# Tying a chunk's transposes behind the next chunk's gate product on TensorE

## The chip, the cores and the metric

One core of one Trainium2 chip runs the kernel. The metric is the time of one execution on the device, in microseconds; a run's number is a median over executions. TensorE is PE in the profile (its weight loads are PEld), VectorE is DVE, ScalarE is ACT, GpSimd is POOL, and SP is the engine whose queue starts the loads.

## The reference

Two decoder layers on 256 tokens of width 1024, all in float32. The first has two kinds of attention and a dense feed-forward part, the second a gated recurrence and then a mixture of experts. Only the last concerns the change: each token goes to the two best of eight experts, and an expert is a gated feed-forward part of width 3584.

```python
def swiglu(u, w_gate, w_up, w_down):
    return (jax.nn.silu(u @ w_gate) * (u @ w_up)) @ w_down

def moe_swiglu(u, w_router, w_gate, w_up, w_down):
    ...
    for e in range(N_EXPERTS):
        y = swiglu(t, w_gate[e], w_up[e], w_down[e]).astype(F32)
        out = out + gates[:, e:e + 1] * y
```

## The kernel before

**A product in three parts.** float32 values are split into a high and a low part. `mm3` (L100) makes one product out of three matmuls: high by high (L101), high by low weights (L102), low by high weights (L103). `split` (L88, both instructions on L91) makes the parts of a weight tile: ACT copies the raw tile to `w_hi`, then DVE subtracts to get `w_lo`. One `split` covers 128x1024 values. `w_hi` and `w_lo` have four buffers each, the raw tiles that the loads fill have fourteen.

**A chunk.** The experts' part is cut into 56 chunks, `Job`s: eight experts, seven chunks of 512 inner columns each. An expert sees at most 128 tokens in its slots. One chunk does this:

- `gate` (L1160): the slots' rows by the gate weights, through `into` (L1144). Two loads of 2 MB in all, four splits, and six matmuls of 128x512 for each split, 24 in all, into one PSUM tile `acc`. Then ACT takes the SiLU into `sg` (L1163). I call the four splits of a chunk's gate G1 to G4.
- `up` (L1165): the same with the up weights, splits U1 to U4. Then DVE multiplies into `hm` (L1168), which has one buffer.
- `turn` (L1170): four TensorE transposes of `hm` into the PSUM tile `tp` (L1173). ACT copies them into `hh` (L1177), and DVE subtracts into `hl` (L1178). `hh` and `hl` have one buffer each.
- `down` (L1180): `hh` and `hl` by the down weights, splits D1 to D4, 24 matmuls into the two PSUM tiles `pj`, which are summed over the seven chunks of an expert. After an expert's last chunk `add` (L1194) scales the sum into `y` (L1202) on ACT and adds it to the output by an indirect DMA; these steps wait in the list `later` and are taken up in the middle of the next chunk's products (L1155).

**The order.** `run_jobs` (L1258) writes a software pipeline: gate of chunk j+1, `turn` of chunk j, up of chunk j+1, down of chunk j. So the written order on PE is down(j-1), gate(j+1), transposes(j), up(j+1), down(j). Where a new pair of experts begins (chunks 14, 28 and 42, counted from 0) `fresh` gathers the next slots' rows and calls the `turn` of the chunk before in the middle of that, followed at once by its `down`.

The written order is not yet the order of the queues. When the program is built, a planner goes through it with estimated costs and puts an instruction into its engine's queue as soon as the estimate has it ready, with the order of the code as the priority. So an instruction whose data is early may be queued ahead of ones written before it. On the chip each queue then runs in the order it was given. `tc.issue_after(ins)` adds an order to this: whatever its block writes for the engine of `ins` is queued behind `ins`. It is an order of issue and not a wait for the end of `ins`, and it holds on that engine alone.

Of the kernel before, what the change touches and what calls it, by code (L numbers as in the profile page):

```python
# [18 lines left out]
KT = D // P  # L19
# [20 lines left out]
def tile_trunk(  # L40
# [22 lines left out]
    nc = tc.nc  # L63
# [11 lines left out]
    def bank(tag, bufs=2):  # L75
        return psum.tile([P, 512], F32, name=tag, tag=tag, bufs=bufs)
# [5 lines left out]
    def load(shape, pieces):  # L82
        r = raws.tile([P] + shape, F32, name="raw", tag="raw")
        for dst, src in pieces(r):
            nc.sync.dma_start(out=dst, in_=src)
        return r

    def split(view, shape):  # L88
        hi = subs.tile([P] + shape, F32R, name="w_hi", tag="w_hi")
        lo = subs.tile([P] + shape, F32R, name="w_lo", tag="w_lo")  # L90
        split.last = nc.scalar.activation(hi, view, AF.Copy), nc.vector.tensor_sub(lo, view, f32(hi))  # L91
        return hi, lo
# [7 lines left out]
    def mm3(ps, xh, xl, wh, wl, first, last, chk=False):  # L100
        nc.tensor.matmul(ps, lhsT=xh, rhs=wh, start=first, stop=False, skip_group_check=chk)  # L101
        nc.tensor.matmul(ps, lhsT=xh, rhs=wl, start=False, stop=False, skip_group_check=chk)  # L102
        nc.tensor.matmul(ps, lhsT=xl, rhs=wh, start=False, stop=last, skip_group_check=chk)  # L103

    def pair_load(w, c0, c1, k):
        wv = [w_.rearrange("(kt p) c -> p kt c", p=P) for w_ in w]
# [2 lines left out]
    def pair_steps(xh, xl, w, c0, c1, ps, late=False, raw=None, ready={}):  # L109


        box = {}

        def step(k):
            if k % 4 == 0:
                box["r"] = raw if raw and k == 0 else pair_load(w, c0, c1, k)
            if k % 2 == 0:
                box["w"] = ready[k] if k in ready else split(box["r"][:, k % 4:k % 4 + 2], [2, 2, 256])
            wh, wl = box["w"]
            box[k] = wh[:, k % 2], wl[:, k % 2]  # L120
            if not late or k >= KT // 2:
                part(k, 0)
                part(k, 1)
            elif k == KT // 2 - 1:
                for t in range(NT):
                    for j in range(KT // 2):
                        part(j, t)

        def part(k, t):
            mm3(ps[t], xh[:, k, TOK[t]], xl[:, k, TOK[t]], *box[k], k == 0, k == KT - 1)  # L130

        return [(1.3, lambda k=k: step(k)) for k in range(KT)]

    def col_steps(xh, xl, w, c0, ps):

        wv = w.rearrange("(kt p) c -> p kt c", p=P)
        box = {}

        def step(k):
            if k == 0:  # L140
                box["r"] = load([KT, 256], lambda r: [(r, wv[:, :, c0:c0 + 256])])
            if k % 4 == 0:
                box["w"] = split(box["r"][:, k:k + 4], [4, 256])
            wh, wl = box["w"]
            for t in range(NT):
                mm3(ps[:, t * 256:(t + 1) * 256], xh[:, k, TOK[t]], xl[:, k, TOK[t]], wh[:, k % 4], wl[:, k % 4],
                    k == 0 and t == 0, k == KT - 1, chk=True)

        return [(0.65, lambda k=k: step(k)) for k in range(KT)]

    def row_steps(xh, xl, wv, ks, acc, first, last):

        box = {}

        def step(k, t):
            if k % 2 == 0 and t == 0:
                box["r"] = load([2, D], lambda r: [(r, wv[:, k:k + 2, :])])
            if t == 0:
                box["w"] = split(box["r"][:, k % 2], [D])
            wh, wl = box["w"]  # L160
            for c in range(2):
                mm3(acc[t][c], xh[:, k, TOK[t]], xl[:, k, TOK[t]], wh[:, HALF[c]], wl[:, HALF[c]], k == first, k == last)

        return [(1.3, lambda k=k, t=t: step(k, t)) for k in ks for t in range(NT)]
# [115 lines left out]
    def to_T(src, xh, xl, t, k0, k1, scale=None, s0=0, gain=None):  # L280
        for k in range(k0, k1, 4):
            n = min(4, k1 - k)
            ps = bank("tp")
            for i in range(n):
                nc.tensor.transpose(out=ps[:, i * P:(i + 1) * P], in_=src[:, (k + i - s0) * P:(k + i - s0 + 1) * P], identity=ident)
            pv = ps[:, :n * P].rearrange("p (a b) -> p a b", b=P)
            oh, ol = xh[:, k:k + n, TOK[t]], xl[:, k:k + n, TOK[t]]
            if gain is not None:
                for i in range(n):
                    g = cols[:, gain + k + i:gain + k + i + 1]  # L290
                    last = (nc.scalar.activation(oh[:, i], pv[:, i], AF.Copy, scale=g),
                            nc.vector.scalar_tensor_tensor(ol[:, i], pv[:, i], g, f32(oh[:, i]), op0=ALU.mult, op1=ALU.subtract))
            elif scale is None:
                last = nc.scalar.activation(oh, pv, AF.Copy), nc.vector.tensor_sub(ol, pv, f32(oh))  # L294
            else:
                last = (nc.scalar.activation(oh, pv, AF.Copy, scale=scale),
                        nc.vector.scalar_tensor_tensor(ol, pv, scale, f32(oh), op0=ALU.mult, op1=ALU.subtract))
        return last

    def x_tiles():  # L300
        return (xts.tile([P, KT, S], F32R, name="xh", tag="xh"), xts.tile([P, KT, S], F32R, name="xl", tag="xl"))

    def norm_T(hgs, gain, acc, into=None):

        xh, xl = into or x_tiles()
        rs = []
        for t in range(NT):
            for c in range(2):
                nc.vector.tensor_add(h[t][:, HALF[c]], acc[t][c], h[t][:, HALF[c]])
                nc.vector.tensor_mul(hgs[t][:, HALF[c]], h[t][:, HALF[c]], gain[:, HALF[c]])  # L310
            r, pw = rms(t)
            rs.append(r)
            for c in range(2):
                to_T(hgs[t], xh, xl, t, 4 * c, 4 * c + 4)
        return xh, xl, rs, pw
# [45 lines left out]
    with tc.tile_pool(name="att", bufs=2) as att, tc.tile_pool(name="atc", bufs=1) as atc:  # L361
# [7 lines left out]
        xh, xl = x_tiles()  # L369
        last = to_T(h[0], xh, xl, 0, 0, 8, gain=GAIN_A)  # L370
        with behind(last):
            ready = {k: split(first[:, k:k + 2], [2, 2, 256]) for k in (0, 2)}
        with behind(split.last):
            last = to_T(h[1], xh, xl, 1, 0, 8, gain=GAIN_A)
# [248 lines left out]
        xh, xl, rx, pw = norm_T([att.tile([P, D], F32, name="wide", tag="sc") for t in range(NT)], gain_f, acc)  # L623
# [5 lines left out]
    with tc.tile_pool(name="ffn", bufs=2) as ffn:  # L629
# [5 lines left out]
        class Chunk:  # L635
# [4 lines left out]
            def into(self):  # L640
                self.pg = [bank("pj") for _ in range(2)]
                return feature_steps(xh, xl, (ffn_w_gate[0], ffn_w_up[0]), self.ch * 256, self.pg)
# [49 lines left out]
        prev = None  # L692
        for ch in range(NCH):
# [10 lines left out]
            prev = cur  # L704
        prev.down()
        xh, xl, rx, pw = norm_T([ffn.tile([P, D], F32, name="wide", tag="wide") for t in range(NT)], gain_h, acc)
# [427 lines left out]
    class Job:  # L1134
# [9 lines left out]
        def into(self, w):  # L1144
            rows = self.rows()
            ps = [bank("acc", 4) for _ in rows]
            for k0 in (0, 4):
                r = load([4, 512], lambda r: [(r, w[:, k0:k0 + 4, self.ch * 512:(self.ch + 1) * 512])])
                for i in range(0, 4, 2):
                    wh, wl = split(r[:, i:i + 2], [2, 512])  # L1150
                    for j in range(2):
                        k = k0 + i + j
                        for p_, (xh, xl, es) in zip(ps, rows):
                            mm3(p_, xh[:, k, es], xl[:, k, es], wh[:, j], wl[:, j], k == 0, k == KT - 1)
                    if later and k0 + i:  # L1155
                        with tc.issue_after(split.last[0].ins):
                            later.pop(0)()
            return ps
# [99 lines left out]
    def run_jobs(jobs):  # L1258

        prev = None  # L1260
        for job in jobs + [None]:
            if job and job.fresh:
                job.fresh(job.shared, prev.turn)
                prev.down()
                prev = None
            if job:
                job.gate()
            if prev:
                prev.turn()
            if job:  # L1270
                job.up()
            if prev:
                prev.down()
            prev = job

    jobs = []
    for e in range(NE):
# [11 lines left out]
        for ch in range(NCH):  # L1289
            kind = {(0, 0): FirstJob, (NE - 1, NCH - 1): LastJob}.get((e, ch), Job)  # L1290
            jobs.append(kind(
                ch, shared, slice((e % 2) * P, (e % 2 + 1) * P), (moe_w_gate[0, e], moe_w_up[0, e], moe_w_down[0, e]), e % 2,
                fresh if e in (2, 4, 6) and ch == 0 else None))
    run_jobs(jobs)


# [5 lines left out]
    with tc.If(most > P):  # L1302
        ecur = mc.tile([P, 1], F32, name="ecur")
        nc.vector.memset(ecur, 0.0)
        with tc.For_i(0, NE, 1) as e:
# [16 lines left out]
            for src, dst in ((nh, xg2[0]), (nl, xg2[1])):  # L1322
                for k0 in range(0, KT, 4):
                    pt = bank("tp")
                    for i in range(4):
                        k = k0 + i
                        for t in range(NT):
                            nc.tensor.matmul(pt[:, i * P:(i + 1) * P], lhsT=src[t][:, k * P:(k + 1) * P], rhs=oh2[:, t],
                                             start=(t == 0), stop=(t == NT - 1))
# [50 lines left out]
```

## Time and profile before

| | |
|---|---|
| median of 3 runs | 1488.56 us (1488.22 to 1489.09) |
| the profiled execution, its own time | 1489.99 us |
| its span in the profile | 1488.3 us |
| TensorE, matmuls | 1453.3 us busy, 98% of the span |
| TensorE, weight loads | 1216.6 us, 82% |
| VectorE | 1213.9 us, 82% |
| ScalarE | 1035.2 us, 70% |
| DMA | 434.05 MB, mean 292 GB/s |
| granted TensorE clock | 0.996 of full speed, mean |

Matmuls are pipelined and their ends are modelled, so TensorE's busy share says little about how near it is to its limit; the distance from one start to the next says more. The experts' chunks fill the span from about 520 us to its end. A line of the timeline shows the start of an instruction, its length, where it stands in the code, and in brackets how long its engine had been idle and who ended that.

### The profile page before, as it was taken

The numbers are of one execution on the slowest core, as the hardware profiler recorded it, in microseconds if no ns is written. First come the engines' busy times: TensorE is split into PE (matmuls) and PEld (weight loads), VectorE is DVE, ScalarE is ACT, GpSimd is POOL, SyncE is SP. The second block draws the span as 40 slices with busy tenths as digits, with TensorE's granted clock in tenths as the row PEclk, the third lists the DMA queues.
The fourth block names the chain that finished last, engine by engine and source line by source line (L and its number), as shares of the span: only waits on it lengthen the run. The fifth ranks groups of instructions, "written<-read, shape, count | busy, mean of one in ns | idle before, by whom it ended". The sixth has DMA issues, their size and how long they took to land.

```text
span 1488.3 us, 20143 instructions
## 1 busy us (share of the span) xinstructions
PE 1453.3 (98%) x7509; PEld 1216.6 (82%) x7509; DVE 1213.9 (82%) x1460; ACT 1035.2 (70%) x1285; POOL 31.9 (2%) x45
## 2 busy tenths in 40 slices
PE   7999999999999999999999999999999999999996
PEld 6887899998889788888888878888877888887885
DVE  7775656557867899999989888889888888888885
ACT  6655544445766688888878777777777777778774
POOL 1000000000000100000000000000000000000000
PEclk9999999999999999999999999999999999999999
DMA  9933355656454499999999999999999999999971
GB/s 315 369 125 114 128 182 187 186 183 183 142 170 142 143 348 365 384 370 385 379 348 376 356 351 395 360 353 360 374 367 373 381 366 350 356 371 362 391 262 16
DMA packets 209691, 434.05 MB, mean 292 GB/s; under 512 B 7402, under 2 KB 58642, under 8 KB 209586
## 3 DMA queue, kind: packets, MB, share of 16 engines
q1 hardware_dynamic: 207506, 425.77, 79.6%
q0 software_dynamic: 2080, 6.92, 2.3%
q8 instruction: 61, 1.00, 0.3%
q14 instruction: 44, 0.36, 0.1%
HBM read 427.41 MB, written 5.24 MB: 291 GB/s over the span
## 4 chain that ended last, share of the span: by engine, by line
issue 53%; PE 37%; DMA 5%; DVE 2%; ACT 2%; POOL 0%; SPq 0%; POOLq 0%; ACTq 0%; DVEq 0%
PE acc L101 5%; PE acc L102 5%; PE acc L103 5%; DMA out_dram<-y,idx 4%; PE pj L342 3%; PE pj L344 3%; PE pj L343 3%; PE pj L101 2%; PE pj L103 2%; PE pj L102 2%; DVE w_lo L91 1%; PE pj L760 1%; PE pj L761 1%; PE pj L762 1%; PE tp L556 1%
## 5 line engine op out<-in xcount | busy, mean ns | idle before, releaser
L91 DVE TENSOR_TENSOR w_lo<-raw,w_hi 128x1024 fp32r<-128x1024 f32 x810 | 956.8, 1221 | 169.2 <-ACT w_hi L91 153.5
L91 ACT ACTIVATE w_hi<-raw 128x1024 fp32r<-128x1024 f32 x810 | 830.0, 1057 | 248.4 <-PE acc L103 82.9
L102 PE MATMUL acc<-w_lo,xgh 128*128 128x512 f32 x904 | 357.9, 396 | 0.0
L101 PE MATMUL acc<-w_hi,xgh 128*128 128x512 f32 x904 | 354.2, 392 | 1.0 <-ACT xgh L294 1.0
L103 PE MATMUL acc<-w_hi,xgl 128*128 128x512 f32 x904 | 353.2, 391 | 0.0
L102 PEld LDWEIGHTS acc<-w_lo,xgh 128*128 128x128 f32 x904 | 169.6, 188 | 51.8 <-DVE w_lo L91 14.6
L101 PEld LDWEIGHTS acc<-w_hi,xgh 128*128 128x128 f32 x904 | 169.8, 188 | 37.1 <-ACT xgh L294 1.2
L103 PEld LDWEIGHTS acc<-w_hi,xgl 128*128 128x128 f32 x904 | 169.8, 188 | 33.0
L102 PE MATMUL pj<-w_lo,hh 128*128 128x512 f32 x448 | 177.8, 397 | 0.0
L103 PE MATMUL pj<-w_hi,hl 128*128 128x512 f32 x448 | 174.9, 390 | 0.0
L101 PE MATMUL pj<-w_hi,hh 128*128 128x512 f32 x448 | 158.1, 391 | 0.7 <-ACT hh L1177 0.5
L101 PEld LDWEIGHTS pj<-w_hi,hh 128*128 128x128 f32 x448 | 84.1, 188 | 19.6 <-ACT hh L1177 0.9
L103 PEld LDWEIGHTS pj<-w_hi,hl 128*128 128x128 f32 x448 | 84.2, 188 | 16.3
L102 PEld LDWEIGHTS pj<-w_lo,hh 128*128 128x128 f32 x448 | 84.2, 188 | 16.3
L342 PE MATMUL pj<-xh,w_hi 128*128 128x256 f32 x320 | 90.8, 284 | 0.6 <-DVE hm L677 0.6
L343 PE MATMUL pj<-xl,w_hi 128*128 128x256 f32 x320 | 90.5, 283 | 0.0
L344 PE MATMUL pj<-xh,w_lo 128*128 128x256 f32 x320 | 90.5, 283 | 0.0
L1163 ACT ACTIVATE sg<-acc 128x512 f32<-128x512 f32 x55 | 32.9, 598 | 52.8 <-PE acc L103 52.8
L1177 ACT ACTIVATE hh<-tp 128x512 fp32r<-128x512 f32 x56 | 33.4, 596 | 49.8 <-PE pj L102 43.4
L342 PEld LDWEIGHTS pj<-xh,w_hi 128*128 128x128 f32 x320 | 61.4, 192 | 1.2 <-DVE hm L677 0.8
L343 PEld LDWEIGHTS pj<-xl,w_hi 128*128 128x128 f32 x320 | 61.4, 192 | 0.4
L344 PEld LDWEIGHTS pj<-xh,w_lo 128*128 128x128 f32 x320 | 61.4, 192 | 0.0
(300 smaller groups left out, 1594.3 us busy)
## 6 DMA issues: line engine op xcount, KB each, us to landing
raw<-in_moe_w_gate_dram SPq DMA_DIRECT2D x112, 1024.0 KB, 7.4
raw<-in_moe_w_up_dram SPq DMA_DIRECT2D x112, 1024.0 KB, 7.9
raw<-in_moe_w_down_dram SPq DMA_DIRECT2D x110, 1024.0 KB, 7.6
raw<-in_ffn_w_gate_dram SPq DMA_DIRECT2D x22, 512.0 KB, 3.8
raw<-in_ffn_w_up_dram SPq DMA_DIRECT2D x22, 512.0 KB, 4.8
raw<-in_ffn_w_down_dram SPq DMA_DIRECT2D x11, 1024.0 KB, 4.8
raw<-in_hgrn_w_in_dram SPq DMA_DIRECT2D x10, 1024.0 KB, 5.5
raw<-in_attn_w_in_dram SPq DMA_DIRECT2D x16, 512.0 KB, 9.3
```

What stands on the lines that cost most here:

```text
L91: split.last = nc.scalar.activation(hi, view, AF.Copy), nc.vector.tensor_sub(lo, view, f32(hi))
L101: nc.tensor.matmul(ps, lhsT=xh, rhs=wh, start=first, stop=False, skip_group_check=chk)
L102: nc.tensor.matmul(ps, lhsT=xh, rhs=wl, start=False, stop=False, skip_group_check=chk)
L103: nc.tensor.matmul(ps, lhsT=xl, rhs=wh, start=False, stop=last, skip_group_check=chk)
L342: nc.tensor.matmul(o, lhsT=wh[:, i, j], rhs=xh[:, k], start=k == 0 and j == 0, stop=False, skip_group_check=True)
L343: nc.tensor.matmul(o, lhsT=wh[:, i, j], rhs=xl[:, k], start=False, stop=False, skip_group_check=True)
L344: nc.tensor.matmul(o, lhsT=wl[:, i, j], rhs=xh[:, k], start=False, stop=k == KT - 1, skip_group_check=True)
L556: nc.tensor.matmul(po[:, j * 64:(j + 1) * 64], lhsT=pT[:, kb, j, :], rhs=v[:, kb, j * 64:(j + 1) * 64], start=(j == 0 and kb == 0), stop=( ...
L760: nc.tensor.matmul(o, lhsT=wh[:, k], rhs=xh[:, k], start=first, stop=False, skip_group_check=True)
L761: nc.tensor.matmul(o, lhsT=wh[:, k], rhs=xl[:, k], start=False, stop=False, skip_group_check=True)
L1163: nc.scalar.activation(self.sg, ps, AF.Silu)
L1177: nc.scalar.activation(self.hh, ptv, AF.Copy)
```

## The change

`mm3` hands back its last matmul, `into` keeps it, and `run_jobs` writes the four transposes of `prev.turn()` in a block that queues what it puts on PE behind the last matmul of the next chunk's gate product. `turn` also writes `hh` for ACT and `hl` for DVE; those get no such order. Where there is no next chunk (the last one), and in the gathers of `fresh`, nothing is tied.

```diff
     def mm3(ps, xh, xl, wh, wl, first, last, chk=False):
...
-        nc.tensor.matmul(ps, lhsT=xl, rhs=wh, start=False, stop=last, skip_group_check=chk)
+        return nc.tensor.matmul(ps, lhsT=xl, rhs=wh, start=False, stop=last, skip_group_check=chk)
...
-                            mm3(p_, xh[:, k, es], xl[:, k, es], wh[:, j], wl[:, j], k == 0, k == KT - 1)
+                            self.last = mm3(p_, xh[:, k, es], xl[:, k, es], wh[:, j], wl[:, j], k == 0, k == KT - 1)
...
             if job:
                 job.gate()
-            if prev:
+            if prev and job:
+                with tc.issue_after(job.last.ins):
+                    prev.turn()
+            elif prev:
                 prev.turn()
```

## Rows read from the trace of the kernel before

**Rows 1.** The page: busy time, share and instructions by engine.

```profile
PE 1453.3 (98%) x7509; PEld 1216.6 (82%) x7509; DVE 1213.9 (82%) x1460; ACT 1035.2 (70%) x1285; POOL 31.9 (2%) x45
```

**Rows 2.** By stretch: length, PE, PEld, DVE, ACT, POOL, clock, DMA share, GB/s.

```profile
600.00:700.00 100.00, 100.00 (x454) 82.76 (x453) 92.72 (x84) 81.84 (x86) 1.69 (x1) 1.00 1.03 380
...
1100.00:1200.00 100.00, 100.00 (x446) 80.41 (x445) 88.16 (x83) 76.13 (x84) 1.82 (x1) 1.00 1.02 373
```

**Rows 3.** Who waited for whom, whole span: total us, times, longest.

```profile
ACT hh L1177 <- PE pj L102: 43.4, 30, 1.5
...
PEld acc L102 <- DVE w_lo L91: 14.6, 41, 0.4
```

**Rows 4.** Waits of SP's load queue, 560 to 1430 us: total, times, longest.

```profile
SPq L85 <- DVE w_lo L91: 734.9, 302, 6.6
```

**Rows 5.** Tile hm, the transposes: min/median/max ns, first and last start.

```profile
L1173 PE MATMUL tp<-ident,hm x224: 270/272/274, 526.9 to 1466.8; 128*128 128x128 f32 x112
```

**Rows 6.** ACT's timeline in an early chunk: start, length, instruction, idle before.

```profile
592.95 1.06 ACT L91 ACTIVATE w_hi<-raw 128x1024 fp32r<-128x1024 f32 x1 [0.30 <-PE acc L103]
594.32 0.60 ACT L1163 ACTIVATE sg<-acc 128x512 f32<-128x512 f32 x1 [0.30 <-PE acc L103]
594.81 0.59 ACT L1177 ACTIVATE hh<-tp 128x512 fp32r<-128x512 f32 x1
```

**Rows 7.** PE's timeline over the same early chunk.

```profile
583.23 0.39 PE L101 MATMUL pj<-w_hi,hh 128*128 128x512 f32 x1
...
594.12 0.60 PE L1173 MATMUL tp<-ident,hm 128*128 128x128 f32 x4
594.47 0.48 PE L101 MATMUL acc<-w_hi,xgh 128*128 128x512 f32 x1
...
600.02 0.39 PE L101 MATMUL pj<-w_hi,hh 128*128 128x512 f32 x1
```

**Rows 8.** ACT's timeline in a late chunk, the last but one.

```profile
1441.97 0.60 ACT L1163 ACTIVATE sg<-acc 128x512 f32<-128x512 f32 x1 [1.30 <-PE acc L103]
...
1453.41 0.60 ACT L1177 ACTIVATE hh<-tp 128x512 fp32r<-128x512 f32 x1 [1.45 <-PE pj L102]
1453.90 3.89 ACT L91 ACTIVATE w_hi<-raw 128x1024 fp32r<-128x1024 f32 x4
1459.09 0.60 ACT L1163 ACTIVATE sg<-acc 128x512 f32<-128x512 f32 x1 [1.30 <-PE acc L103]
```

**Rows 9.** PE's timeline in the late chunk before it.

```profile
1430.40 0.62 PE L101 MATMUL pj<-w_hi,hh 128*128 128x512 f32 x2
...
1432.22 0.60 PE L1173 MATMUL tp<-ident,hm 128*128 128x128 f32 x4
...
1447.50 0.62 PE L101 MATMUL pj<-w_hi,hh 128*128 128x512 f32 x2
```

**Rows 10.** Timeline of ACT where the order turns from early to late.

```profile
833.82 0.60 ACT L1163 ACTIVATE sg<-acc 128x512 f32<-128x512 f32 x1 [1.66 <-PE acc L103]
834.31 0.59 ACT L1177 ACTIVATE hh<-tp 128x512 fp32r<-128x512 f32 x1
834.79 4.90 ACT L91 ACTIVATE w_hi<-raw 128x1024 fp32r<-128x1024 f32 x5
```

**Rows 11.** Timeline of PE at the same place.

```profile
833.62 0.60 PE L1173 MATMUL tp<-ident,hm 128*128 128x128 f32 x4
...
839.79 0.62 PE L101 MATMUL pj<-w_hi,hh 128*128 128x512 f32 x2
```

**Rows 12.** Timeline of DVE at the same place.

```profile
834.94 0.69 DVE L1178 TENSOR_TENSOR hl<-tp,hh 128x512 fp32r<-128x512 f32 x1 [1.52 <-ACT hh L1177]
835.88 3.50 DVE L91 TENSOR_TENSOR w_lo<-raw,w_hi 128x1024 fp32r<-128x1024 f32 x3 [0.26 <-ACT w_hi L91]
```

**Rows 13.** Timeline of ACT: two gate ends with an expert's output scaling between.

```profile
868.51 0.60 ACT L1163 ACTIVATE sg<-acc 128x512 f32<-128x512 f32 x1 [1.30 <-PE acc L103]
...
885.88 0.60 ACT L1163 ACTIVATE sg<-acc 128x512 f32<-128x512 f32 x1 [0.91 <-PE acc L103]
```

## The prediction

> **What bounds the kernel now.** I read the page's first part, then the busy time by stretch, then the waits, and then the timeline of PE beside that of ACT, chunk by chunk. The page has PE at 98% [rows 1], and in the experts' part it is busy without a gap in an early and in a late stretch alike, at full granted clock [rows 2]. By that share the two stretches are equal. By the number of matmuls they are not: 454 in 100 us early, 446 late. So the starts have to be read. Early, the 48 matmuls of a down and a gate product take 10.89 us, 0.227 each [rows 7], and a chunk's 72 take 16.3 of its 16.79 us. PE's stream bounds this part, and the rest of a chunk, some 0.5 us, is what an order in the queues can be worth.
>
> The other engines are near, though not ahead. The loads wait only for `w_lo` to free a raw tile [rows 4], and no engine's wait in this part is put down to a load. PE waits for split weights 41 times, 14.6 us in all [rows 3]. The transposes' own cost is four starts in 0.35 us, from 594.12 to 594.47 [rows 7].
>
> The change has something to act on because there are two orders in this trace. In the early chunks PE has the transposes behind the gate product, as the change wants it, and ACT has `hh` right behind `sg` with no idle time [rows 6, 7]. In the late ones they stand eight matmuls into the down product [rows 9]; then `hh` is queued on ACT ahead of the next chunk's G3 and waits 1.45 us for the end of that down product, since it has one buffer [rows 8]. That wait is 43.4 us over 30 chunks [rows 3]. The turn is at the 19th `sg`, at 833.82 [rows 10], the last `sg`, at 1459.09 [rows 8], is the 55th: 36 late intervals. Early intervals are 16.79 to 16.82, plain late ones 17.10 (1430.40 to 1447.50) [rows 7, 9].
>
> **What the change moves.** It adds no instruction and no semaphore wait. There are 56 sets of four transposes [rows 5]; 55 have a next chunk and three of these are in the gathers, so 52 are tied. Of these, 18 lie before the turn and stand there already: those chunks keep their time. 34 sets move some 40 matmuls back on PE. No load is moved; the loads that follow a moved `w_lo` go with it.
>
> *The transposes on PE:* 0.35 us taken from the down product, 0.35 put behind the gate. Sum nothing.
>
> *The wait of `hh` at the end of the down product:* gone, since `hh` cannot be ready before the next gate is over, and by then the down product has long been. ACT then goes from G2 straight to G3, 1.5 us earlier. But ACT was off the path there: what PE loses at G3 is small, as the late sum below shows. Late next on that engine is the gate's `sg`.
>
> *`hh` and `hl` in their new place:* this decides. ACT runs in order, and all that is queued behind `hh` is later by its 0.49 us. Which splits are these? The chunk at the turn shows it. Its transposes still come behind the gate, as in every tied chunk; but `sg` has already come ahead of U3: ACT idles 1.66 us for the gate's end, takes `sg`, then `hh`, and only then five splits in a row [rows 10]. (Early, three splits of the up product precede `sg` and ACT idles 0.30 before it [rows 6]; the 1.36 us more of idle time here is the place of one split, 1.06 and its wait.) So the queue lost its lead before any transpose left its place, and just at the border of two loads: the planner takes the second load of each product to be late. The transposes that went ahead are a consequence of this; tying them does not give the lead back. I therefore take the chunk at the turn as the pattern of all tied late chunks.
>
> Its price is in its rows. From the transposes to the first matmul of the down product it takes 6.17 us, 833.62 to 839.79 [rows 11]; an early chunk takes 5.90 [rows 7]. The 0.27 between them is mostly the wait for the `w_lo` of U3, which begins at 835.88 behind `hl` [rows 12]. For the down and the gate product I take the early 10.89, as nothing is left in them that waits. Sum: 6.17 + 10.89 = 17.06 against 17.10, or 0.04 less in each of 33 plain intervals: 1.3 us.
>
> *Three intervals with an expert's scaling:* 17.37 [rows 13]. After the change between 17.06 and 17.33; the scaling waits for the down product as `hh` did, so part stays. I take 17.2: 0.5 us.
>
> *The last chunk* is not tied, and one set moves past the gate before it: nothing.
>
> Together 1.8 us. On the profiled execution's own 1489.99 that is 1488.2; the median of the runs is 1.43 lower, and from it the sum gives **1486.8**. Bounds of this case: a tied chunk of 17.00 (ACT's shift half hidden under the moved transposes) with the scaling free gives 33 x 0.10 + 3 x 0.31 = 4.2, thus 1484.4; one of 17.12 (0.02 lost at the down product's first split) gives 1489.0.
>
> The Trainium skill (TensorE: Matmul & The Clock Gate, section Back-to-back issue gap) has streams of weight load and matmul at 512 columns sustained at about 131 ns each. By that a chunk's 72 would be 9.4 us, an estimate from that page, PE would have 7 us to spare in each chunk, and no order on it could matter. This trace has 0.227 us [rows 7], and the argument goes by the trace.
>
> **The rivals.**
>
> *Early order everywhere.* The tie lets the planner keep U3 ahead of `sg`, or at least `hh` behind U3. Then a late chunk takes 16.81: 33 x 0.29 + 3 x 0.56 = 11.3 us, 1477.3. For it: 18 chunks in this order, and the loads keep up at 380 GB/s there as at 373 late [rows 2]. Against it: the lead was lost while the transposes were still in place [rows 10]. Chance 0.18.
>
> *`sg` and `hh` get ahead of U2 as well.* This is the slower one. At the turn the first `w_lo` behind `hh` is done near 837.05 (835.88 and a third of 3.50) [rows 12]; if it were that of U2, PE would want it at about 835.56, the seventh matmul's time after the transposes plus one. It would wait 1.5 us where U3 now costs 0.2: 1.3 x 34 = 44, 1531. It decides from the point where the planner has the gate's end before the second split of the up product. Against it: the 1.30 us of idle time before a late `sg` [rows 8] is the place of one missing split, not of two. With lesser delays at the same place, that give over 1491.5, chance 0.11.
>
> *No change in the late chunks at all*, because what the tie frees at G3 comes back at U3 in full: that is the low end of my own case, and I count it there. That the change does nothing to the queue is true of the 18 early sets only [rows 5, 6].
>
> **How the numbers follow.** About 0.2%, 3.0 us, is what a measurement of this kernel can tell from no change. My case has 0.71; its bounds reach past 1485.6 at the low end, which I give 0.13 of the 0.71. Faster: 0.18 + 0.13 = 0.31. Slower 0.11. The same: 0.58. The range has to reach to the early order, as my own case alone, 1484.4 to 1489.0, holds less than 0.8; it goes from 1477.0 to 1489.2.
>
> **What would show it.** Right: the waits lose the row of `hh` for `pj`; every `hh` follows `sg` on ACT without idle time and is followed by five splits; `sg` idles about 1.6 us; the transposes to the down product take 6.17, down and gate 10.89. Wrong towards faster: three splits of the up product ahead of `sg`, intervals of 16.8. Wrong towards slower: one split ahead of `sg`, or PE waiting for `w_lo` behind the transposes for over 0.3 us.

## The result, and the profile after

The changed kernel takes **1501.4 us** (median of 4 runs, 1500.59 to 1502.52) against 1488.52 for the kernel before beside it (4 runs, 1488.22 to 1489.09). The ratio is 1.0087, with an interval of 1.0069 to 1.0104: slower by 12.9 us, where the sum gave 1486.8 and the range ended at 1489.2. The profiled execution took 1502.08 us with a span of 1500.3; before, the span was 1488.3. The mean granted clock is 0.995 against 0.996, and 1.00 in both stretches below as in [rows 2]: the clock is not the cause.

The page of the changed kernel, which answers to [rows 1]:

```profile
PE 1461.6 (97%) x7509; PEld 1216.3 (81%) x7509; DVE 1212.8 (81%) x1460; ACT 1045.3 (70%) x1285; POOL 31.9 (2%) x45
```

The number of instructions is the same on every engine. PE's busy time has grown by 8.3 us without one more matmul, so PE's share is no reading of what it does.

By stretch, with the columns of [rows 2]:

```profile
600.00:700.00 100.00, 100.00 (x454) 82.75 (x454) 92.77 (x84) 82.03 (x86) 1.69 (x1) 1.00 1.03 378
...
1100.00:1200.00 100.00, 99.37 (x434) 78.44 (x433) 86.75 (x81) 78.12 (x84) 1.83 (x1) 1.00 1.00 369
```

The early stretch has not moved: 454 matmuls. The late one has lost 12 of 446. The reader should look at that count rather than at the 99.37.

The waits over the whole span (total us, times, longest), which answer to [rows 3]:

```profile
ACT sg L1163 <- PE acc L103: 63.5, 55, 1.7
DVE hl L1178 <- ACT hh L1177: 50.4, 51, 1.5
...
PEld pj L102 <- DVE w_lo L91: 16.9, 32, 0.5
...
PEld acc L102 <- DVE w_lo L91: 15.2, 40, 0.8
```

The waits of `hh` for `pj` are gone, as forecast, all but one of 1.5 us. The row of `acc` for `w_lo` is about what it was (15.2 after 14.6): it is mostly the wait for U3 in the late chunks, which both kernels have. The row `PEld pj L102 <- DVE w_lo L91` is **new**: 32 waits of half a microsecond in the down product, for the low part of a weight tile.

ACT's timeline at the turn, of a late chunk, and at the last `sg`, against [rows 8] and [rows 10]:

```profile
833.41 0.60 ACT L1163 ACTIVATE sg<-acc 128x512 f32<-128x512 f32 x1 [1.66 <-PE acc L103]
...
1435.64 0.60 ACT L1163 ACTIVATE sg<-acc 128x512 f32<-128x512 f32 x1 [1.67 <-PE acc L103]
1436.13 0.59 ACT L1177 ACTIVATE hh<-tp 128x512 fp32r<-128x512 f32 x1
1436.61 4.92 ACT L91 ACTIVATE w_hi<-raw 128x1024 fp32r<-128x1024 f32 x5
...
1453.13 0.60 ACT L1163 ACTIVATE sg<-acc 128x512 f32<-128x512 f32 x1 [1.66 <-PE acc L103]
...
1470.59 0.60 ACT L1163 ACTIVATE sg<-acc 128x512 f32<-128x512 f32 x1 [1.67 <-PE acc L103]
```

This is the pattern of [rows 10]: `sg` after 1.66 or 1.67 us of idle time, `hh` with none, five splits in a row. In every tied late chunk `hh` follows `sg` in this way; only where an expert's scaling comes between is the idle time ahead of `sg` shorter, 0.88 us. But from one `sg` to the next it is 17.49 us, not 17.06; the plain late intervals are 17.45 to 17.54. Between the `sg` of the turn (833.82 before, 833.41 after) and the last one (1459.09, 1470.59), the same 36 intervals take 625.27 us before and 637.18 after. That is 11.9 of the 12.0 us between the spans, so the loss lies in the late chunks.

PE's timeline of that chunk, from its down product on, against [rows 9]:

```profile
1441.65 0.62 PE L101 MATMUL pj<-w_hi,hh 128*128 128x512 f32 x2
...
1443.01 0.61 PE L101 MATMUL pj<-w_hi,hh 128*128 128x512 f32 x2
1443.73 0.50 PE L102 MATMUL pj<-w_lo,hh 128*128 128x512 f32 x1
1444.06 0.39 PE L103 MATMUL pj<-w_hi,hl 128*128 128x512 f32 x1
...
1447.49 0.39 PE L101 MATMUL acc<-w_hi,xgh 128*128 128x512 f32 x1
...
1452.93 0.60 PE L1173 MATMUL tp<-ident,hm 128*128 128x128 f32 x4
1453.29 0.48 PE L101 MATMUL acc<-w_hi,xgh 128*128 128x512 f32 x1
...
1459.10 0.61 PE L101 MATMUL pj<-w_hi,hh 128*128 128x512 f32 x2
```

The parts: down 1441.65 to 1447.49, 5.84 us; gate 5.44; the transposes 0.36; the up product 5.81. The last two make the 6.17 of [rows 11], as taken, and the gate is one half of 10.89. The down product is not: it is 0.40 longer. Within it, D2's two products with the high part begin at 1443.01. Two starts at 0.227 later, at 1443.46, its first product with the low part should begin. It begins at 1443.73, 0.27 late, and the product behind it follows after 0.33 in place of 0.227.

The weight load of that product, and DVE's timeline there:

```profile
1443.73 0.19 PEld L102 LDWEIGHTS pj<-w_lo,hh 128*128 128x128 f32 x1 [0.53 <-DVE w_lo L91]
```

```profile
1436.76 0.69 DVE L1178 TENSOR_TENSOR hl<-tp,hh 128x512 fp32r<-128x512 f32 x1 [1.50 <-ACT hh L1177]
1437.70 3.50 DVE L91 TENSOR_TENSOR w_lo<-raw,w_hi 128x1024 fp32r<-128x1024 f32 x3 [0.25 <-ACT w_hi L91]
1441.85 0.69 DVE L1168 TENSOR_TENSOR hm<-acc,sg 128x512 f32<-128x512 f32 x1 [0.65 <-PE acc L103]
1442.46 10.30 DVE L91 TENSOR_TENSOR w_lo<-raw,w_hi 128x1024 fp32r<-128x1024 f32 x9
```

Behind `hl` come three low parts, U3, U4 and D1. Then DVE idles 0.65 us in front of `hm`, which needs the end of the up product, though D2's high part is there by about 1440.5 (an estimate: the fourth of the five splits that ACT began at 1436.61). Only behind `hm`, from 1442.46, does it make the low part of D2, and with a third of 3.50 us for one it is done near 1443.63. PE's load begins 0.10 later.

Now the same place in the trace of the kernel before. PE's timeline:

```profile
1448.86 0.62 PE L101 MATMUL pj<-w_hi,hh 128*128 128x512 f32 x2
1449.32 0.60 PE L1173 MATMUL tp<-ident,hm 128*128 128x128 f32 x4
1449.67 0.48 PE L102 MATMUL pj<-w_lo,hh 128*128 128x512 f32 x1
```

And DVE's:

```profile
1447.70 0.69 DVE L1168 TENSOR_TENSOR hm<-acc,sg 128x512 f32<-128x512 f32 x1 [0.65 <-PE acc L103]
1448.31 5.76 DVE L91 TENSOR_TENSOR w_lo<-raw,w_hi 128x1024 fp32r<-128x1024 f32 x5
```

The same `hm`, with the same 0.65 us ahead of it and D2's low part behind it, done near 1449.46 (a fifth of 5.76 after 1448.31). But here PE had the four transposes in hand from 1449.32 to 1449.67. They stood in the very hole that the late low part leaves, and the waits of that trace have no row `PEld pj L102 <- DVE w_lo L91`.

### The profile page after: what moved, and what is told of

Its sections match the earlier page's. It is cut to its first block, busy times and chain, and to the rows that moved or that the text cites. A ratio compares the mean times of both kernels' runs of the same rounds, so it can differ in the third digit from the quotient of the medians.

```text
span 1500.3 us, 20078 instructions
## 1 busy us (share of the span) xinstructions
PE 1461.6 (97%) x7509; PEld 1216.3 (81%) x7509; DVE 1212.8 (81%) x1460; ACT 1045.3 (70%) x1285; POOL 31.9 (2%) x45
## 4 chain that ended last, share of the span: by engine, by line
issue 53%; PE 36%; DMA 5%; DVE 2%; ACT 2%; POOL 0%; SPq 0%; POOLq 0%; ACTq 0%; DVEq 0%
PE acc L101 5%; PE acc L102 5%; PE acc L103 5%; DMA out_dram<-y,idx 4%; PE pj L342 3%; PE pj L344 3%; PE pj L343 3%; PE pj L101 2%; PE pj L103 2%; PE pj L102 2%; DVE w_lo L91 1%; PE pj L760 1%; PE pj L761 1%; PE pj L762 1%; PE tp L556 1%
## 5 line engine op out<-in xcount | busy, mean ns | idle before, releaser
L91 DVE TENSOR_TENSOR w_lo<-raw,w_hi 128x1024 fp32r<-128x1024 f32 x810 | 954.2, 1222 | 137.3 <-ACT w_hi L91 121.5
L91 ACT ACTIVATE w_hi<-raw 128x1024 fp32r<-128x1024 f32 x810 | 840.6, 1061 | 283.1 <-PE acc L103 102.4
L102 PE MATMUL acc<-w_lo,xgh 128*128 128x512 f32 x904 | 356.9, 395 | 0.7 <-DVE w_lo L91 0.7
L102 PEld LDWEIGHTS acc<-w_lo,xgh 128*128 128x128 f32 x904 | 170.0, 188 | 47.8 <-DVE w_lo L91 15.2
L102 PE MATMUL pj<-w_lo,hh 128*128 128x512 f32 x448 | 178.5, 398 | 3.4
L101 PE MATMUL pj<-w_hi,hh 128*128 128x512 f32 x448 | 152.9, 391 | 0.7 <-ACT hh L1177 0.5
L102 PEld LDWEIGHTS pj<-w_lo,hh 128*128 128x128 f32 x448 | 84.1, 188 | 33.3 <-DVE w_lo L91 16.9
L1178 DVE TENSOR_TENSOR hl<-tp,hh 128x512 fp32r<-128x512 f32 x56 | 38.7, 692 | 50.5 <-ACT hh L1177 50.4
```

Of the source, the lines that this page charges most:

```text
L1178: nc.vector.tensor_sub(self.hl, ptv, f32(self.hh))
```

## The experiments

**Theory A**, formed from these rows: in the late chunks D2's low part is behind `hm` on DVE. Before, the transposes filled PE's wait for it and so cost nearly nothing; moved behind the gate they cost their whole 0.35 us, and the wait lies bare. **Its rival**: the loss belongs to the new order on ACT and DVE (`hh` and `hl` ahead of U3 and all later splits), wherever the transposes stand. What each theory expects is on record with each run. Four of the kernels (D2's low part ahead of `hm`, the wait laid bare, the wait in early chunks too, the early order everywhere) ran beside 13 runs of the kernel before with a median of 1488.37 us, the other three beside 13 with 1488.04.

### The wait taken away: D2's low part ahead of `hm`

To the changed kernel; `up` no longer writes the product, and `down` of the chunk ahead does, behind D2's low part on DVE:

```diff
+        def mul(self):
             self.hm = moe.tile([P, 512], F32, name="hm", tag="hm", bufs=1)
-            nc.vector.tensor_mul(self.hm, ps, self.sg)
+            nc.vector.tensor_mul(self.hm, self.pu, self.sg)
...
+                    if then and i0 + i == 1:
+                        with tc.issue_after(split.last[1].ins):
+                            then()
...
-                prev.down()
+                prev.down(job.mul) if job else prev.down()
```

> The changed kernel, with one order more: hm is written in the down product of the chunk before and queued on DVE behind the low part of D2. All else stands as in the changed kernel. Theory A (the transposes had covered PE's wait for the low part of D2, which DVE makes only after hm): without hm ahead of it D2 is ready in time, a late chunk's down product falls from 5.84 to about 5.47 us, a plain late chunk from 17.47 to about 17.09, 34 such chunks give 13 us, so about 1488.5 us (1486 to 1491). Theory B (the cost is in the new place of the transposes, hh and hl between gate and up): nothing moves, 1499 to 1503 us.

Measured: 1488.06 us (10 runs), ratio to before 0.9997 (0.9985 to 1.001). The down product takes 5.44 and the plain late interval 17.05 to 17.10. DVE's and PE's timelines of this kernel in a late chunk:

```profile
1027.17 4.63 DVE L91 TENSOR_TENSOR w_lo<-raw,w_hi 128x1024 fp32r<-128x1024 f32 x4 [0.26 <-ACT w_hi L91]
1031.71 0.68 DVE L1170 TENSOR_TENSOR hm<-acc,sg 128x512 f32<-128x512 f32 x1
1032.31 9.44 DVE L91 TENSOR_TENSOR w_lo<-raw,w_hi 128x1024 fp32r<-128x1024 f32 x8
```

```profile
1032.43 0.61 PE L101 MATMUL pj<-w_hi,hh 128*128 128x512 f32 x2
1032.88 0.39 PE L102 MATMUL pj<-w_lo,hh 128*128 128x512 f32 x1
```

Four low parts now stand ahead of `hm`, the idle 0.65 is gone, and D2's low product starts 0.45 after its high ones, without a wait. One instruction's place on DVE takes back all the loss, with the transposes still behind the gate and ACT's order that of the changed kernel. So the rival falls, and the intervals, 17.06 on the mean, are what the prediction had summed. From the `sg` at the turn to the last one this kernel takes 623.80 us, 1.5 less than the 625.27 of the kernel before: the gain that was forecast, 1.8, nearly comes once this one wait is away.

### The wait laid bare in the kernel before

To the kernel before; the orders on ACT and DVE stay, and the late chunks' transposes are put four matmuls further into the down product, behind D2 instead of in its middle:

```diff
+                    if then and i0 + i == 1:
+                        with tc.issue_after(m.ins):
+                            t = then()
+                        behind_t.enter_context(tc.issue_after(t.ins))
...
-                prev.turn()
+                prev.parts() if hasattr(prev, "pt") else prev.turn()
...
+                if job and n >= 19 and not (nxt and nxt.fresh):
...
+                    prev.down(then)
```

> The kernel before, untied, with the orders of ACT and DVE unchanged; in the late chunks alone the transposes are moved by four matmuls, from ahead of D2's low-part products to behind them, inside the down product. Theory A: the wait for the low part of D2 lies bare, the down product grows by 0.35 to 0.40 in some 34 chunks, about 1501 us (1498 to 1503). Theory B: transposes, hh and hl are where they were, so 1488 to 1489.5 us.

Measured: 1502.28 us (4 runs), ratio 1.0095 (1.0078 to 1.0112), plain interval 17.47. PE's timeline:

```profile
1052.30 0.61 PE L101 MATMUL pj<-w_hi,hh 128*128 128x512 f32 x2
1053.02 0.50 PE L102 MATMUL pj<-w_lo,hh 128*128 128x512 f32 x1
...
1054.05 0.60 PE L1177 MATMUL tp<-ident,hm 128*128 128x128 f32 x4
```

It is 0.72 us from the high to the low product, as in the changed kernel, and the transposes' own time comes on top. Four matmuls' worth of distance costs as much as forty did. It is not how far they move that costs, but that they leave this place.

### The hole filled again with work that nobody reads

To the changed kernel; in 35 late chunks D2's products are written out, and four transposes of the identity, which no one reads, stand between the high and the low ones. In the plain chunks this adds work and changes nothing else; at the gathers of `fresh` the queues come out a little differently (two intervals in a row of 27.50 and 10.88 us, where the changed kernel has 27.19 and 11.76):

```diff
+                        pt = bank("tp")
+                        with tc.issue_after(m.ins):
+                            for n in range(4):
+                                m = nc.tensor.transpose(out=pt[:, n * P:(n + 1) * P], in_=ident, identity=ident)
+                        with tc.issue_after(m.ins):
+                            for c in range(2):
+                                nc.tensor.matmul(sh["py"][c], lhsT=xh, rhs=wl[:, HALF[c]], start=False, stop=False)
```

> The changed kernel with work added: in 35 late chunks four more transposes (of the identity, read by nobody) stand where the kernel before had its own, between D2's high-part and low-part products. Theory A (PE waits there anyway): they fill the wait, the down product goes from 5.84 to 5.44 + 0.02 + 0.35 + 0.12 = 5.93, about 0.09 more in each chunk, 3 us in all: 1503 to 1506 us. Theory B (transposes cost what they take on PE, wherever they stand): 0.35 to 0.48 in each, 12 to 17 us: 1513 to 1519 us.

Measured: 1503.85 us (4 runs), ratio 1.0107 (1.009 to 1.0123). PE's timeline:

```profile
1053.51 0.62 PE L1191 MATMUL pj<-w_hi,hh 128*128 128x512 f32 x2
1053.97 0.60 PE L1195 MATMUL tp<-ident 128*128 128x128 f32 x4
1054.32 0.48 PE L1198 MATMUL pj<-w_lo,hh 128*128 128x512 f32 x1
```

The down product takes 5.93 us where the changed kernel's takes 5.84: 0.35 us of transposes cost 0.09. (0.09 x 35 = 3.2 us; the medians lie 2.5 apart, from runs on two occasions, and each of the two gathers takes some 0.6 less.) This is what the transposes cost where they stood before, and it prices the change: 0.36 at the new place less 0.09 at the old is 0.27 of the 0.37 a chunk. The rest, some 0.1, is about what the product behind them loses at its start (the last section has it); that the rest is this was not tested.

### The wait put into early chunks too

To the kernel of the next experiment (early order everywhere): D2's low part is queued behind `hm` on DVE, early chunks too.

```diff
-            nc.vector.tensor_mul(self.hm, ps, self.sg)
+            self.mul = nc.vector.tensor_mul(self.hm, ps, self.sg)
...
-                    wh, wl = split(r[:, i], [D])
+                    with tc.issue_after(mul.ins) if mul and i0 + i == 1 else ExitStack():
+                        wh, wl = split(r[:, i], [D])
...
-                prev.down()
+                prev.down(job.mul) if job else prev.down()
```

> As the kernel with U3 first, but the low part of D2 is queued on DVE behind hm in every chunk, the early ones too. Theory A: the down product of every chunk, early ones too, takes about 5.84 in place of 5.44, the chunks about 17.2 in place of 16.81, and with 52 of them the kernel is about 20 us above the one with U3 first: 1494 to 1500 us. Theory B: the same as the one with U3 first.

Measured: 1502.05 us (4 runs), ratio 1.0086 (1.0069 to 1.0103). The down product takes 5.84 to 5.88 in 48 chunks, early and late; those at the gathers and the last one do not have the wait. An early chunk's PE and DVE:

```profile
587.63 0.61 PE L101 MATMUL pj<-w_hi,hh 128*128 128x512 f32 x2
588.35 0.50 PE L102 MATMUL pj<-w_lo,hh 128*128 128x512 f32 x1
```

```profile
586.48 0.69 DVE L1173 TENSOR_TENSOR hm<-acc,sg 128x512 f32<-128x512 f32 x1 [1.48 <-PE acc L103]
587.08 5.76 DVE L91 TENSOR_TENSOR w_lo<-raw,w_hi 128x1024 fp32r<-128x1024 f32 x5
```

The wait appears in chunks that never had it, with the same 0.72 from high to low. The total is 23.8 us over its base of 1478.29, above the time I gave, 1494 to 1500. The wait has the size expected: from the first `sg` to the 55th it is 941.87 us against 921.70 in the base, 20.2 more, or 0.42 for each of the 48 chunks. But the first `sg` itself is 4.1 us later in this profiled execution (528.90 against 524.79). Ahead of it the two differ in the granted clock (0.95 against 0.98 from 100 to 200 us, 0.98 against 1.00 from 300 to 400), and not in the edit, which touches only the experts' chunks.

### The early order everywhere

To the changed kernel; `sg`, and `hh` behind it, are queued on ACT behind the split of U3, and the tie of the transposes stays:

```diff
+                    if then and k0 + i == 4:
+                        with tc.issue_after(split.last[0].ins):
+                            then()
...
+                def mid(job=job, prev=prev):
+                    if not isinstance(job, FirstJob):
+                        job.silu()
+                    if prev:
+                        prev.parts()
...
-                job.up()
+                job.up(mid)
```

> The changed kernel, with sg and hh queued on ACT behind the high part of U3. The planner then also puts hl behind U3 and hm behind D2 on DVE. Theory A: both waits go, that of U3 behind the transposes (0.27 us of 0.38) and that of D2 (0.40); late chunks take the early 16.81 and the kernel 1476 to 1480 us. Theory B: only the wait at U3 goes, 36 times 0.27, thus 1491 to 1493 us.

Measured: **1478.29 us** (4 runs), ratio 0.9942 (0.9925 to 0.9959). This is faster than both kernels. ACT's and DVE's timelines late in the span:

```profile
1036.82 1.06 ACT L91 ACTIVATE w_hi<-raw 128x1024 fp32r<-128x1024 f32 x1 [0.30 <-PE acc L103]
1038.19 0.60 ACT L1168 ACTIVATE sg<-acc 128x512 f32<-128x512 f32 x1 [0.30 <-PE acc L103]
1038.69 0.59 ACT L1188 ACTIVATE hh<-tp 128x512 fp32r<-128x512 f32 x1
1039.16 2.01 ACT L91 ACTIVATE w_hi<-raw 128x1024 fp32r<-128x1024 f32 x2
```

```profile
1040.26 3.50 DVE L91 TENSOR_TENSOR w_lo<-raw,w_hi 128x1024 fp32r<-128x1024 f32 x3 [0.26 <-ACT w_hi L91]
1044.10 0.69 DVE L1173 TENSOR_TENSOR hm<-acc,sg 128x512 f32<-128x512 f32 x1 [0.34 <-PE acc L103]
```

This is [rows 6] in a late chunk. With U3 already split, the three low parts behind `hl` are U4, D1 and D2, so D2's is made ahead of `hm` and nothing waits for it. The wait for U3 goes as well: the row `PEld acc L102 <- DVE w_lo L91` is 2.0 us in 5 waits, after 14.6 in 41 before. Intervals are 16.79 to 16.82 to the end. It is near the time of the prediction's first rival (1477.3), by another edit: the tie alone does not bring it.

### The same without the tie

```diff
-                with tc.issue_after(job.last.ins):
-                    prev.turn_only()
+                prev.turn_only()
```

> The kernel with U3 first, but without the tie of the transposes: the planner puts two of the four behind D3's high-part products and two behind the first product of the next gate. Theory A: where sg and hh stand behind U3, no low part is late, nothing is left to cover, and the tie is worth nothing of its own: 1477 to 1480 us, within 2 us of the tied one. Theory B (the tie itself is what gains there): back near 1488 us.

Measured: 1478.6 us (4 runs), ratio 0.9941 (0.9924 to 0.9957). The planner now puts two of the transposes into D3 and two into the next G1; the late intervals are 16.81 to 16.85. The two kernels ran beside different runs of before, and their ratios are alike. The tie, which is all of the change studied here, gives nothing that these runs can tell once ACT's order is right.

### Where the order turns

Why does the planner lose the early order at the 19th chunk? To the kernel before, with ten raw tiles instead of 14:

```diff
-NRAW = 14
+NRAW = 10
```

> The kernel before with ten raw tiles in place of fourteen, nothing else written differently. If the planner loses its lead because it takes the loads to be slower than the chip has them, a smaller store is used up sooner: the turn comes some six or seven chunks earlier, each costs 0.29 us, and 1489.5 to 1492 us come out, with PE still never waiting for a load. If the turn has to do with the transposes or with the place in the expert's seven chunks, it stays near 834 us, and so does the time, at 1488 to 1489.

Measured: 1491.92 us (10 runs, 1488.31 to 1494.6), ratio 1.0021 (1.0007 to 1.0035). The 11th `sg` is the last one with the early order of [rows 6], 0.30 us of idle time and `hh` behind it. ACT's timeline there, with the `hh` of the next chunk:

```profile
696.44 0.60 ACT L1163 ACTIVATE sg<-acc 128x512 f32<-128x512 f32 x1 [0.30 <-PE acc L103]
711.23 0.60 ACT L1177 ACTIVATE hh<-tp 128x512 fp32r<-128x512 f32 x1 [2.36 <-PE tp L1173]
```

That `hh` comes ahead of its `sg`, at 713.75, as in a late chunk. So the turn is at the 12th `sg`, where the kernel before has it at the 19th: fewer tiles to load ahead bring it sooner. In the experts' part no engine's wait was put down to a load in this run either. This fits a planner that takes the loads to be slower than they are and turns when the lead of the raw tiles is used up; the late order would then answer a lateness that this chip does not show. That reading of the planner was tried at this one size alone and is not shown beyond it.

## Why the prediction failed

- **"For the down and the gate product I take the early 10.89, as nothing is left in them that waits."** This is the step that failed. Measured: 5.84 + 5.44 = 11.28. The 5.44 of the gate holds; the down product had a wait left, which its rows hid because the transposes were lying over it. In the trace of before the sign was there: in [rows 9] the transposes come at 1432.22, eight matmuls of 0.227 behind the start of the down product. What the product behind them needs (D2's low part), and what is ahead of that on DVE (`hm`), would have told of the wait.
- **"0.35 us taken from the down product, 0.35 put behind the gate. Sum nothing."** The same error from the other end. The second half is right (0.36 at 1452.93). The first is not: taking them out of the down product shortens it by 0.09 and not by 0.35, since a bare wait stands in their place. Before, the down product with the transposes in it took 5.93, as the filled one does, 0.49 over a clean one; after, without them, it takes 5.84, 0.40 over a clean one. The chunk shown takes 17.45 from one down product to the next, where the one before (1447.50 to 1464.62) took 17.12. Its balance is -0.09 at the down product, +0.36 for the transposes behind the gate, and +0.06 in the gate and up products (11.25 without the transposes, 11.19 before): 0.33 together. The mean over the plain late intervals, 17.47 against 17.10, is 0.37 more.
- **`hh`'s wait gone, five splits behind it, some 1.6 us of idle time before `sg`, 6.17 from the transposes to the down product**: right, the 6.17 to 0.01 us. Choosing the chunk at the turn as the pattern was right too. But that chunk could not show the fault. Its own down product, from 839.79 on, already lay behind the turn, and I took the transposes to the down product from it and the rest from the early chunk, which has U3 ahead and therefore D2's low part ahead of `hm`. The measurement had to be carried on to the next `sg` of one kind of chunk.
- **18 early chunks keep their time**: right; 16.79 to 16.82.
- **Three intervals with scaling, 17.2**: 17.49 to 17.50, with the same wait in their down products. The count of 33 plain intervals beside them was too high: four of the 36 lie at two gathers (26.62 and 11.75, 26.64 and 11.79 before) and the one behind the turn took 17.58, so 28 were plain. At 0.04 each that is 0.2 us of the sum, and not what failed.
- **The early order everywhere** as a result of the tie did not come. Its price was nearly right, 11.3 us forecast and 10.1 measured with another edit (1478.29 against 1488.37 before), and it was right that the tie has no hold on ACT.
- **`sg` and `hh` ahead of U2**, the slower rival, did not come either. That rival looked for the loss at the place where the transposes arrive; it was at the place that they left.

That the bare wait makes the loss is shown from four sides: taken away (1488.06), laid bare without the tie (1502.28), filled (0.09 for 0.35 us of work), and put where it never was (5.84 to 5.88 in early chunks). What is argued and not shown is the last 0.1 us or so of the 0.37 in a chunk, and why the planner turns.

## What to carry to other kernels

Before an instruction is moved off a busy queue, look at the instruction behind it: trace its operands back through the queues that make them, and see whether the moved one stands in a wait that it hides. A table of waits names only waits that are bare: the row of 32 waits here came up only when the transposes had left. Where a kernel's queue order comes from a plan with estimates, an order that changes midway for no reason that the trace shows is worth a trial of its own: here two instructions' place on ACT was worth 10 us, and with it right the place of the transposes on PE was worth nothing that these runs can tell.

## What the runs showed of the hardware

In these traces an interruption of PE's stream costs more than itself. Behind the first product after the wait for D2's low part the next starts 0.33 us later (1443.73 to 1444.06), and behind the first after the transposes 0.31 (1453.29 to 1453.60), where 0.227 is usual: some 0.1 us for each, whether PE had waited or had worked on something else. In the filled hole the wait and the transposes share one such start (1054.32 to 1054.63, 0.31), and together they cost 0.49 us (5.93 less 5.44), where the bare wait alone costs 0.40.

The Trainium skill (TensorE: Matmul & The Clock Gate, section Part 4: PE-mode transpose) gives about 390 ns for a transpose of 128x128 in bf16 by itself, and about 275 ns for one in a kernel. The 272 ns of [rows 5], here for float32, are near the second figure as the length of one. What four of them took from PE's stream here is 0.36 us in all, 1452.93 to 1453.29, and 0.09 where they filled a wait.
